# Two stacked blocks on one core: the norms' sums on VectorE, rescaling and broadcasts later in the second block, and the first block's side work in another order

## The chip, the core and the metric

One core of a Trainium2 chip runs the whole program in one launch. Its engines are TensorE (PE in the profile, with its weight loads as PEld), VectorE (DVE), ScalarE (ACT), GpSimd (POOL) and SyncE (SP, which here issues the weight DMAs). Each takes its own instructions strictly in order. The metric is the device time of one execution in microseconds; lower is better. TensorE's clock has two levels in the traces, 1.2 and 2.4 GHz; the profile gives the granted clock of a stretch as a share of the higher one.

## The reference

Two different blocks of two layers each work on one sequence of 256 tokens with 1024 features. Everything is fp32.

```python
def first_block(x, ...):
    for i in range(DEPTH):                       # 2 layers
        h = rmsnorm(x, norm_mix[i])
        q, k, v, cb, cc, cx, u, g = jnp.split(h @ w_in[i], IN_SPLITS, axis=-1)
        y_attn = sliding_window_attention(rope(q), rope(k), v, attn_sinks[i]) @ w_attn_o[i]
        y_conv = (cb * short_conv(cc * cx, conv_w[i])) @ w_conv_o[i]
        ys = gelu(s5_ssm(u, ...))
        y_ssm = (ys * sigmoid(ys @ w_ssm_glu[i])) @ w_ssm_o[i]
        gates = sigmoid(g + b_gate[i]).reshape(b, l, 3, D_MODEL)
        x = x + (gates[0] * y_attn + gates[1] * y_conv + gates[2] * y_ssm) @ w_mix_o[i]
        gt, up = jnp.split(rmsnorm(x, norm_ffn[i]) @ w_ffn_in[i], 2, axis=-1)
        x = x + (silu(gt) * up) @ w_ffn_out[i]
    return rmsnorm(x, norm_final)

def second_block(x, ...):
    for l in range(DEPTH):                       # 2 layers
        h = rmsnorm(h_in, norm_mix_w[l]) @ w_in[l]   # q, k, v, g_ret, z, xbc, dt, gates
        # retention: 4 heads, 256 keys, 512 values, rotary; rms norm per head, times silu(g_ret)
        # ssd: causal conv of width 4, silu, chunked scan over 4 groups of 8 heads,
        #      times silu(z), rms norm per group
        # merged = sigmoid(gate_ret) * o_ret + sigmoid(gate_ssd) * o_ssd;  h += merged @ w_o[l]
        # h += swiglu(rmsnorm(h, norm_ffn_w[l]))
    return rmsnorm(h, final_norm_w)
```

## The kernel before

**Products.** The activations stand in `X` with features on partitions (8 tiles of 128 features by 256 tokens). Each fp32 product is made of three products in a rounded format: a weight chunk of 512 KB lands as `raw`, ScalarE rounds it to `wh` (`cp`), VectorE subtracts to get the rest `wl` (`sub`), and the input is split likewise into `xh` and `xl`, which lie in one tile `xhl`. `fm` gives a result with features on partitions (24 matmuls with 256 columns for a chunk of four 128-row pieces), `tm` one with tokens on partitions. `raw` has 4 buffers, `wh` and `wl` 5 together, PSUM has 4 `mm` tiles for products, 3 `ax` tiles for everything else and one `st` tile.

**Norms.** `Norm` spares a wait for the norm: the products after it run on `X` times the gain, without the factor of the token. `pair(mp)` makes `xhl` for two feature tiles as soon as they are known, and `squares(mp)` squares them on ScalarE (tile `sq`) and adds the two halves into `acc`. `steps` sums `acc` over partitions on TensorE into `st`; rsqrt on VectorE, in some fourteen instructions of 128x2, gives `rsc` (a factor for each token, tokens on partitions); `rowbc` spreads it along the free dimension: VectorE writes a diagonal `dg`, TensorE multiplies it by ones into an `ax` tile, ScalarE copies that to `rsb`. Results made before that are scaled when they leave PSUM. `rescale` later makes a new `xhl` from `X` times `rsb`, so that the rest of the products need no factor: four muls of 128x512 (tile `sq`), each with two roundings on ScalarE and two on VectorE. In six norms `acc` is added on POOL for `mp` 0 to 2 (five adds of 128x256) and on VectorE for `mp` 3; in the first one all are on VectorE.

**First block.** `layer1` runs over `w_in`: two `fm` for `u` (of the S5), a `tm` for k and v, in whose middle (`mid_kv`) the norm is finished and `spread_u` copies the scaled `u` into `U2` with 32 copies of 32x128, half of them on ScalarE and half on VectorE; a `tm` for q; `rescale`; for each half of the conv branch `pc_`, `px` and `pb`; then gates, the S5 output, attention, and `w_mix_o`. Between products `bg.tick` advances a side list. In layer 0 that is `PLAN_0`, the making of the S5 tables for four groups b: `A1`, `A2` (powers of the state's rotation, on POOL, into tile `W`), `PC`, `CP` (powers on VectorE into tile `CP`), `BP` (POOL), `BX` (ScalarE copies `BP` into a padded tile `BX` and `CP` into `W`), `WK` (transposes of `BX`, two `ax` tiles, copied into `W`; then 16 small products of `W` by `BX` into a third `ax` tile), `KK` (16 copies of that into `W`), `M1` (the state products and the scan) and `M2` (the output `py` in an `ax` tile, then a tanh form of gelu: a square on ScalarE, two steps on VectorE, a tanh on ScalarE, and `Y` on VectorE, which frees `py`). The tables of layer 1 (`PLAN_1`) are made beside the feed-forward part of layer 0, and the scheduler may begin them earlier.

**Second block.** In `layer2` each of four heads has products for q, k and v, then one for `sg` (`silu2`: a tanh and a multiply), and `head_tail` later. Head 0's q, k and v run without the norm's factor, then `rescale`, then `sg`. The ssd part ends each of four groups with a norm over the group: rsqrt and `rowbc` again.

**Order.** Code order sets each engine's order, but a list scheduler moves what has a priority: `high_priority(offset=URGENT)`, with URGENT = 200, lets the instructions written inside it go ahead by that many. `pinned` keeps what it is given in code order, behind the last instruction of each engine that it finds in a look back:

```python
for i in reversed(seq[-300:]):
    last.setdefault(i.engine, i)
```

The lines that a reader needs: L104 is `tt` (all two-input steps of VectorE and POOL), L116 the two-step form of VectorE, L119 `ts`, L129 `act` (all of ScalarE), L135 `mmu`, L790 the memset of a `W` tile, L828 the transposes of `WK`.

## Time and profile before

| what | value |
|---|---|
| median of 3 runs | 2252.89 us (2251.32 to 2256.33) |
| profiled execution | 2256.99 us, span 2255.2 us |
| mean granted TensorE clock | 0.986 |
| PE busy | 2178.6 us, 97% |
| DVE busy | 1548.2 us, 69% |
| ACT busy | 1221.7 us, 54% |
| POOL busy | 199.6 us, 9% |
| HBM read | 386.88 MB, 175 GB/s over the span |

The times in the rows are counted from the start of the span. A matmul's own time in a row includes its way through the pipeline, so neighbours overlap; how fast they follow each other is read from a stretch, as its length over the count. A group such as "x4" is several instructions one after the other, with their time together. A wait names the engine and the tile whose event came last.

### The profile page before, as it was taken

The page shows a single profiled execution, that of the slowest core. Times are in us where ns is not written, and L with a number is a line of the kernel's source. Part 1 is how long each engine was busy: PE and PEld are TensorE (multiplying, and loading weights), DVE is VectorE, ACT ScalarE, POOL GpSimd, SP SyncE. Part 2 cuts the span into 40 slices and gives each one's busy share as a digit, 9 for nine tenths or more (in the row PEclk, how much of TensorE's full clock was granted, in tenths as well). Part 3 has the DMA queues.
Part 4 walks back from the last instruction along what each step waited for, and adds up shares of the span by engine and source line. Part 5 has one row for each costly group of instructions (what it writes and reads, how often), then busy time and mean ns, then how long its engine had stood idle before and what let it go on. Part 6 is the DMA issues. An engine that isn't in the chain of part 4 may idle for free. (4 is left out here: it accounts for less than half of the span.)

```text
span 2255.2 us, 36864 instructions
## 1 busy us (share of the span) xinstructions
PE 2178.6 (97%) x14368; PEld 1971.0 (87%) x14368; DVE 1548.2 (69%) x2515; ACT 1221.7 (54%) x1949; POOL 199.6 (9%) x359
## 2 busy tenths in 40 slices
PE   7999969999999999999999999999999999999997
PEld 6898958899999889888999989889888899989886
DVE  7766646568756655776568887556766668887554
ACT  6666537645555444444476755444444477655442
POOL 5810244001000000100000000000100000000000
PEclk9899989999999999999999999999999999999999
DMA  6443537766645655555566646555555566456553
GB/s 184 148 127 122 168 120 240 233 207 220 195 136 178 191 186 173 162 186 165 160 201 202 187 157 192 186 174 183 171 166 177 161 200 199 149 185 196 185 178 103
DMA packets 343935, 397.75 MB, mean 176 GB/s; under 512 B 27988, under 2 KB 276688, under 8 KB 342736
## 3 DMA queue, kind: packets, MB, share of 16 engines
q1 hardware_dynamic: 342816, 394.48, 56.0%
q8 instruction: 113, 1.85, 0.3%
q10 hardware_dynamic: 592, 0.79, 0.1%
q14 instruction: 62, 0.51, 0.1%
q0 software_dynamic: 352, 0.11, 0.0%
HBM read 386.88 MB, written 8.45 MB: 175 GB/s over the span
## 5 line engine op out<-in xcount | busy, mean ns | idle before, releaser
L104 DVE TENSOR_TENSOR wl<-raw,wh 128x1024 fp32r<-128x1024 f32 (+1 forms) x698 | 850.1, 1221 | 516.5 <-ACT wh L129 488.4
L129 ACT ACTIVATE wh<-raw 128x1024 fp32r<-128x1024 f32 (+1 forms) x698 | 727.8, 1047 | 822.5 <-PE mm L135 663.4
L135 PE MATMUL mm<-xhl,wh 128*128 128x256 f32 x3616 | 672.2, 287 | 4.9 <-ACT xhl L129 3.2
L135 PE MATMUL mm<-wh,xhl 128*128 128x512 f32 (+1 forms) x2176 | 645.3, 381 | 3.0 <-DVE xhl L116 1.3
L135 PEld LDWEIGHTS mm<-xhl,wh 128*128 128x128 f32 x3616 | 567.7, 192 | 11.5 <-ACT xhl L129 4.1
L135 PE MATMUL mm<-xhl,wl 128*128 128x256 f32 (+1 forms) x1808 | 515.3, 285 | 3.8 <-DVE wl L104 3.8
L135 PEld LDWEIGHTS mm<-wh,xhl 128*128 128x128 f32 x2176 | 398.7, 190 | 81.3 <-issue 4.3
L135 PE MATMUL mm<-wl,xhl 128*128 128x512 f32 (+1 forms) x1088 | 410.4, 377 | 5.5 <-DVE wl L104 5.5
L135 PEld LDWEIGHTS mm<-xhl,wl 128*128 128x128 f32 (+1 forms) x1808 | 347.6, 192 | 5.7 <-DVE wl L104 4.9
L135 PEld LDWEIGHTS mm<-wl,xhl 128*128 128x128 f32 x1088 | 206.8, 190 | 43.2 <-DVE wl L104 6.0
L135 PE MATMUL mm<-hh,wh 128*128 128x512 f32 (+1 forms) x660 | 185.4, 348 | 0.0
L135 PE MATMUL mm<-y,wh 128*128 128x512 f32 (+1 forms) x576 | 182.1, 372 | 1.0 <-DVE y L116 1.0
L135 PE MATMUL mm<-hh,wl 128*128 128x256 f32 x528 | 147.9, 280 | 0.0
L135 PE MATMUL mm<-y,wl 128*128 128x256 f32 x512 | 144.3, 282 | 0.0
L135 PEld LDWEIGHTS mm<-hh,wh 128*128 128x128 f32 x660 | 114.7, 188 | 16.7
L135 PEld LDWEIGHTS mm<-y,wh 128*128 128x128 f32 x576 | 103.8, 188 | 21.9 <-DVE y L116 1.7
L104 POOL TENSOR_TENSOR acc<-sq 128x256 f32<-128x256 f32 x6 | 4.8, 795 | 1245.3 <-ACT sq L129 1245.3
L135 PEld LDWEIGHTS mm<-hh,wl 128*128 128x128 f32 x528 | 99.1, 188 | 0.0
L135 PEld LDWEIGHTS mm<-y,wl 128*128 128x128 f32 x512 | 96.2, 188 | 0.5 <-issue 0.3
L135 PE MATMUL mm<-mg,wh 128*128 128x256 f32 x512 | 90.5, 280 | 0.0
L135 PEld LDWEIGHTS mm<-mg,wh 128*128 128x128 f32 x512 | 78.4, 189 | 0.0
L116 DVE SCALAR_TENSOR_TENSOR ta<-mm,vec,ta 128x255 f32<-128x255 f32 (+2 forms) x144 | 67.2, 476 | 9.5 <-ACT ta L129 9.2
(363 smaller groups left out, 2446.6 us busy)
## 6 DMA issues: line engine op xcount, KB each, us to landing
raw<-in_w_in_dram SPq DMA_DIRECT2D x284, 512.0 KB, 4.3
raw<-in_w_ffn_in_dram SPq DMA_DIRECT2D x88, 512.0 KB, 3.6
raw<-in_w_gate_up_dram SPq DMA_DIRECT2D x88, 512.0 KB, 3.5
raw<-in_w_down_dram SPq DMA_DIRECT2D x42, 512.0 KB, 3.8
raw<-in_w_ffn_out_dram SPq DMA_DIRECT2D x40, 512.0 KB, 3.5
raw<-in_ret_out_dram SPq DMA_DIRECT2D x32, 512.0 KB, 3.8
raw<-in_ssd_out_dram SPq DMA_DIRECT2D x32, 512.0 KB, 3.4
raw<-in_w_mix_o_dram SPq DMA_DIRECT2D x16, 512.0 KB, 3.4
```

Of the source, the lines that this page charges most:

```text
L104: return eng.tensor_tensor(out=o, in0=a, in1=b, op=op)
L116: return V.scalar_tensor_tensor(out=o, in0=a, scalar=s, in1=b, op0=op0, op1=op1)
L129: return SC.activation(out=o, in_=i, func=f, **kw)
L135: return PE.matmul(out=o, lhsT=l, rhs=r, start=start, stop=stop)
```

## The change

Several things change together.

1. `squares` adds all of `acc` on VectorE.
2. At the start a tile `warm` of 128x256 zeros feeds twelve fp32 matmuls into an `ax` tile that nobody reads, ahead of the transposes of the input.
3. In `layer1` the chunks of q's product are given a priority of 250 ahead. `mid_kv` spreads only the first half of `u`; the second half is scaled into a part of `Y2` and spread after the first half of the conv branch. `pc_` of the first half runs on the unscaled `xhl`, and `rsb` is multiplied in when it leaves PSUM; `rescale` and (in layer 0) `params_1` come behind it.
4. `BXs` copies all of `BP` to `BX` first and then `CP` to `W`; the 16 small products go from `WK` to `KK`.
5. The first gate product of the attention branch runs before attention, and the later ones one step earlier; the attention's second pool has two buffers instead of one.
6. In `layer2` head 0's `sg` runs before `rescale`: the tanh takes the factor of the token, and the rest of it goes into `rd` of `head_tail`.
7. The Exp of `al` is pinned, and `pinned` looks back over 2000 instructions instead of 300.
8. In the group norms of the ssd the rsqrt is urgent, and `rowbc` lets one more step pass between `dg` and its product.

```diff
-        for i in reversed(seq[-300:]):
+        for i in reversed(seq[-2000:]):
...
-    def chunk(parts, kn, n):
+    def chunk(parts, kn, n, ahead_by=0):
...
-        for ap, off in parts:
-            nc.sync.dma_start(out=raw[:, :, off:off + ap.shape[1]], in_=ap.rearrange("(k p) c -> p k c", p=128))
-        cp(wh, raw)
-        sub(wl, raw, wh.bitcast(F32))
+        with tc.high_priority(offset=ahead_by):
+            for ap, off in parts:
+                nc.sync.dma_start(out=raw[:, :, off:off + ap.shape[1]], in_=ap.rearrange("(k p) c -> p k c", p=128))
+            cp(wh, raw)
+            sub(wl, raw, wh.bitcast(F32))
...
-    def rowbc(colv, o):
+    def rowbc(colv, o, wait=False):
...
         yield
+        if wait:
+            yield
...
-            eng = V if mp == 3 or self.gain is gfirst else G
             if mp == 0:
                 self.acc = T(sqp, [128, S], "acc")
-                add(self.acc, sq[:, 0], sq[:, 1], eng)
+                add(self.acc, sq[:, 0], sq[:, 1])
             else:
                 for k in range(2):
-                    add(self.acc, self.acc, sq[:, k], eng)
+                    add(self.acc, self.acc, sq[:, k])
...
-            for ri in range(2):
-                t, x = W2[:, ri], z[:, ri]
-                for a in range(2):
-                    r = slice(64 * a, 64 * a + 64)
-                    cp(t[r, :, :, a, :], CP[r, :, ri].rearrange("p i t h -> p t i h"), -1.0 if ri else None)
-                    cp(x[r, :, :, a, :], BP[r, :, ri].rearrange("p i t h -> p t i h"))
+            halves = [(ri, a, slice(64 * a, 64 * a + 64)) for ri in range(2) for a in range(2)]
+            for ri, a, r in halves:
+                cp(z[r, ri, :, :, a, :], BP[r, :, ri].rearrange("p i t h -> p t i h"))
+            for ri, a, r in halves:
+                cp(W2[r, ri, :, :, a, :], CP[r, :, ri].rearrange("p i t h -> p t i h"), -1.0 if ri else None)
...
+        def KK(b):
+            W2, KT = st[b]["w"][1:3]
             pk = axt([128, 128])
...
-        def KK(b):
-            KT, kk = st[b]["w"][2], st[b]["kk"]
...
-        ap2 = st.enter_context(tc.tile_pool(name="att2", bufs=1))
+        ap2 = st.enter_context(tc.tile_pool(name="att2", bufs=2))
...
-            for m2 in range(2):
-                spread_u(m2)
+            scale_u(0)
+            spread_u(0)
+            scale_u(1)
...
-        ps = tm(w, 0, D, XX, mid=lambda: bg.tick(next(steps)))
+        ps = tm(w, 0, D, XX, mid=lambda: bg.tick(next(steps)), ahead_by=250)
...
-        nm.rescale(V if l == 0 else G)
...
-            cp(z, pc_)
+            if m2 == 0:
+                mul(z, pc_, bc(nm.rsb, 2))
+                nm.rescale(V if l == 0 else G)
+            else:
+                cp(z, pc_)
             bg.tick(next(steps))
+            if m2 == 0 and l == 0:
+                pinned(params_1)
...
+            if m2 == 0:
+                spread_u(1)
...
+        g0 = gate(0, 0, p=inner.enter_context(tc.tile_pool(name="g0p", bufs=1)))
...
-            g = gate(0, mp)
+            g, g0 = g0, gate(0, mp + 1) if mp < 3 else None
...
-            act(al, al, AF.Exp)
+            pinned(lambda: act(al, al, AF.Exp))
...
-            ts(rd, rd, 0.5, None, ALU.mult, ALU.bypass)
+            if h == 0:
+                stt(rd, rd, 0.5, nm.rsc, ALU.mult, ALU.mult)
+            else:
+                ts(rd, rd, 0.5, None, ALU.mult, ALU.bypass)
...
+            pg = tm(w, 4096 + 512 * h, D, XX, mid=bg.tick)
             if h == 0:
+                rh = T(sm, [128, 2], "r8")
+                ts(rh, nm.rsc, 0.5, None, ALU.mult, ALU.bypass)
+                silu2(pg, sg, rh)
                 nm.rescale()
-            sg = e["sg"] = T(r2, [128, 2, 512], "sg")
-            silu2(tm(w, 4096 + 512 * h, D, XX, mid=bg.tick), sg)
+            else:
+                silu2(pg, sg)
...
-            rd = rsqrt(ps[:, 0:2], 2, 1.0 / 512)
+            with tc.high_priority(offset=URGENT):
+                rd = rsqrt(ps[:, 0:2], 2, 1.0 / 512)
...
-            yield from rowbc(rd, rdb)
-            yield
+            yield from rowbc(rd, rdb, True)
...
-    warm = ip.tile([128, 1], F32, name="warm")
+    warm = ip.tile([128, 256], F32, name="warm")
     V.memset(warm, 0.0)
-    act(warm, warm, AF.Exp)
+    act(warm[:, 0:1], warm[:, 0:1], AF.Exp)
+    idle = axt()
+    for _ in range(12):
+        mmu(idle[:, 0, :], warm[:, 0:128], warm, True, True)
```

**Where instructions go.** On POOL, before, near the end of layer 0's `w_mix_o`, the adds of its second norm stood between the steps of layer 1's S5 tables (`g`, `BP`, `W`):

```order
L104 TENSOR_TENSOR g_554_3684<-bt_3548,s_cw 128x256
L104 TENSOR_TENSOR g_555_3685<-bt_3548,s_cw 128x256
L104 TENSOR_TENSOR BP_3683<-g_554_3684,g_555_3685 128x4x64
L104 TENSOR_TENSOR acc_3315<-acc_3315,sq_3383 128x256
L104 TENSOR_TENSOR g_554_3684<-bt_3548,s_cw 128x256
L104 TENSOR_TENSOR acc_3315<-acc_3315,sq_3383 128x256
L104 TENSOR_TENSOR g_555_3685<-bt_3548,s_cw 128x256
L104 TENSOR_TENSOR BP_3683<-g_554_3684,g_555_3685 128x4x64
L790 MEMSET W_3695 128x1792
```
After, on VectorE, the same adds stand between the weight rests `wl`, the residual update of `X` and the rounding rests of `xhl`:

```order
L116 SCALAR_TENSOR_TENSOR X<-mm_3402,X 128x512
L104 TENSOR_TENSOR wl_3665<-raw_3663,wh_3664 128x1024
L116 SCALAR_TENSOR_TENSOR xhl_92<-X,vec,xhl_92 128x256 x2
L104 TENSOR_TENSOR acc_3330<-acc_3330,sq_3468 128x256 x2
L104 TENSOR_TENSOR wl_3683<-raw_3681,wh_3682 128x1024
L116 SCALAR_TENSOR_TENSOR X<-mm_3472,X 128x512
L104 TENSOR_TENSOR wl_3775<-raw_3773,wh_3774 128x1024
L116 SCALAR_TENSOR_TENSOR xhl_92<-X,vec,xhl_92 128x256 x2
L104 TENSOR_TENSOR acc_3330<-acc_3330,sq_3538 128x256 x2
L104 TENSOR_TENSOR wl_3793<-raw_3791,wh_3792 128x1024
```
All of them now follow the `xhl` step of their own pair of tiles, and the last two have one `wl` in front of the next rsqrt.

On VectorE, before, in layer 0's product for q, the rest of its last weight chunk (`wl_801`) stood behind the second half of the copies to `U_48_386` and steps of `params_1` (`vec`, `hbg`, `gfm`), and the muls of `rescale` (`sq`) followed:

```order
L1051 COPY U_48_386<-ta_619 32x2x64 x7
L218 COPY vec<-ax_689 128x128
L104 TENSOR_TENSOR g_103_736<-CP_674,s_pw 128x256
L119 TENSOR_SCALAR hbg<-vec 128x48
L104 TENSOR_TENSOR gfm<-vec 128x8
L104 TENSOR_TENSOR gf_108<-vec 128x8
L104 TENSOR_TENSOR g_104_737<-CP_674,s_pw 128x256
L104 TENSOR_TENSOR wl_801<-raw_799,wh_800 128x1024
L104 TENSOR_TENSOR CP_674<-g_103_736,g_104_737 128x4x64
L104 TENSOR_TENSOR sq_821<-X,rsb_508 128x512
```
After, that last chunk is `wl_790`, and it stands ahead of the norm's `dg`, while the scaling of `u` (`ta_614`) comes behind:

```order
L104 TENSOR_TENSOR wl_790<-raw_788,wh_789 128x1024
L116 SCALAR_TENSOR_TENSOR s_hs<-s_hs 128x32
L104 TENSOR_TENSOR nt_506<-nt_506,nv_503 128x2
L119 TENSOR_SCALAR s_hs<-s_hs 128x32
L116 SCALAR_TENSOR_TENSOR ny_505<-nt_506,ny_505 128x2
L476 COPY rsc_502<-ny_505 128x2
L119 TENSOR_SCALAR dg_522<-C,rsc_502 128x128 x2
L119 TENSOR_SCALAR r_93_685<-rsc_502 128x2
L116 SCALAR_TENSOR_TENSOR s_u<-s_hs 128x32
L116 SCALAR_TENSOR_TENSOR s_x<-s_hs 128x32
L104 TENSOR_TENSOR s_pw<-s_mag,s_u 128x32
L104 TENSOR_TENSOR ta_614<-mm_401,rsb_521 128x2x64x4
```
The four `wl` of q have moved in front of the broadcast, and the copies and `params_1` behind the conv product's weights.

On ScalarE, before, in layer 0, the copies for the second S5 group into `W_744` and `BX_515` alternated:

```order
L129 ACTIVATE ta_1203<-mm_1142 128x512
L129 ACTIVATE W_744<-CP_1085 64x20x16
L129 ACTIVATE BX_515<-BP_677 64x16x16
L129 ACTIVATE W_744<-CP_1085 64x20x16
L129 ACTIVATE BX_515<-BP_677 64x16x16 x3
L129 ACTIVATE wh_1531<-raw_1530 128x1024
L129 ACTIVATE W_744<-CP_1085 64x20x16 x2
```
After, all copies into `BX_528` stand ahead of those into `W_733`, and three weight roundings (`wh`) stand before the square `n` of the group before, where two and the conv step `tb` stood:

```order
L129 ACTIVATE ta_1215<-mm_1154 128x512
L129 ACTIVATE BX_528<-BP_673 64x16x16 x4
L129 ACTIVATE W_733<-CP_1081 64x20x16 x2
L129 ACTIVATE wh_1493<-raw_1492 128x1024
L129 ACTIVATE W_733<-CP_1081 64x20x16 x2
L129 ACTIVATE wh_1543<-raw_1542 128x1024
L129 ACTIVATE wh_1577<-raw_1576 128x1024
L129 ACTIVATE n_185_1300<-ax_1287 128x256
```
The first copy into `BX` no longer stands behind a copy that needs `CP`.

## Rows read from the trace of the kernel before

**Rows 1.** The page's busy time by engine and its groups, `busy, mean ns`.
```profile
PE 2178.6 (97%) x14368; PEld 1971.0 (87%) x14368; DVE 1548.2 (69%) x2515; ACT 1221.7 (54%) x1949; POOL 199.6 (9%) x359
...
L104 DVE TENSOR_TENSOR wl<-raw,wh 128x1024 fp32r<-128x1024 f32 (+1 forms) x698 | 850.1, 1221 | 516.5 <-ACT wh L129 488.4
```
**Rows 2.** TensorE's waits: line <- releaser: us in total, times, longest us.
```profile
PE st L135 <- DVE acc L104: 16.9, 1, 16.9
PE mm L135 <- DVE wl L104: 9.3, 6, 5.5
PE ax L135 <- DVE dg L119: 8.3, 5, 3.2
PE ax L135 <- ACT W L129: 6.5, 3, 3.0
...
PE mm L135 <- ACT xhl L129: 3.2, 2, 2.6
PE mm L135 <- ACT ss L129: 2.0, 1, 2.0
...
PE mm L135 <- DVE xhl L116: 1.3, 2, 0.8
```
**Rows 3.** Stretches: us, busy us (x) of PE PEld DVE ACT POOL, PEclk, DMA, GB/s.
```profile
10.00:20.00 10.00, 9.14 (x53) 8.84 (x54) 9.01 (x15) 9.44 (x17) 0.00 (x0) 1.00 1.02 250
20.00:30.00 10.00, 10.00 (x85) 9.88 (x84) 8.71 (x37) 7.04 (x11) 0.00 (x0) 1.00 0.77 244
40.00:50.00 10.00, 4.46 (x15) 3.33 (x14) 9.83 (x25) 4.65 (x14) 9.45 (x21) 0.70 0.14 43
50.00:60.00 10.00, 8.48 (x43) 7.00 (x42) 8.70 (x15) 8.05 (x17) 9.42 (x21) 0.79 0.33 106
90.00:100.00 10.00, 5.43 (x41) 4.94 (x42) 9.24 (x16) 9.17 (x17) 8.99 (x20) 0.76 0.75 237
100.00:110.00 10.00, 10.00 (x73) 9.64 (x65) 3.73 (x5) 8.98 (x26) 6.51 (x12) 0.73 0.10 30
190.00:200.00 10.00, 10.00 (x68) 9.39 (x68) 5.42 (x18) 5.25 (x8) 0.00 (x0) 0.83 0.39 124
280.00:290.00 10.00, 10.00 (x64) 8.84 (x63) 6.72 (x8) 4.33 (x8) 9.30 (x19) 1.00 0.64 205
300.00:310.00 10.00, 2.88 (x9) 2.50 (x10) 3.69 (x10) 0.00 (x0) 5.75 (x12) 0.50 0.06 15
310.00:320.00 10.00, 10.00 (x38) 8.07 (x37) 5.78 (x17) 4.45 (x5) 0.00 (x0) 0.82 0.47 148
```
**Rows 4.** Timeline around 290 us: start, us, instruction, [idle before <-releaser].
```profile
293.32 0.63 ACT L129 ACTIVATE sq<-X 128x512 f32<-128x512 f32 x1 [6.81 <-POOL acc L104]
...
304.62 1.52 POOL L104 TENSOR_TENSOR acc<-acc,sq 128x256 f32<-128x256 f32 x2
...
306.18 0.89 DVE L104 TENSOR_TENSOR acc<-acc,sq 128x256 f32<-128x256 f32 x2 [17.64 <-POOL acc L104]
```
**Rows 5.** Timeline from 45 to 66 us: VectorE, POOL and TensorE.
```profile
45.67 1.63 DVE L104 TENSOR_TENSOR wl<-raw,wh 128x1024 fp32r<-128x1024 f32 x1
...
47.83 1.59 POOL L790 MEMSET W<- 128x1792 f32 x1
...
64.98 0.65 PE L135 MATMUL ax<-W,BX 128*32 128x128 f32 x16
```
**Rows 6.** Timeline of the S5 steps: ScalarE and TensorE near 91, VectorE at 128 us.
```profile
90.34 0.47 ACT L129 ACTIVATE W<-CP 64x320 f32<-64x320 f32 x1 [4.80 <-DVE CP L104]
...
91.96 2.00 PE L828 MATMUL ax<-C,BX 128*128 128x128 f32 x8 [1.55 <-ACT BX L129]
...
128.53 0.42 DVE L116 SCALAR_TENSOR_TENSOR Y<-n,ax 128x256 f32<-128x256 f32 x1 [0.48 <-ACT n L129]
```
**Rows 7.** Timeline of the second block, layer 1: ScalarE and TensorE.
```profile
1586.65 0.23 ACT L129 ACTIVATE al<-al 128x32 f32<-128x32 f32 x1 [4.34 <-DMA al<-in_a_log_dram]
...
1938.59 1.22 PE L135 MATMUL ax<-dg,C 128*128 128x128 f32 x4 [3.21 <-DVE dg L119]
```

35 lines of the change are left out of this document (19 added, 16 removed).

## The prediction

> **What bounds the kernel now.** I read the busy shares first. TensorE is busy for 2178.6 of 2255.2 us [rows 1], so a change that leaves its matmuls alone can give back only two things: the time in which TensorE stands still, and the time in which it runs at 1.2 GHz instead of 2.4. The first is in the view of TensorE's waits by releaser [rows 2]: one wait of 16.9 us for VectorE's `acc`, six for `wl` with 9.3 us together, five for `dg` with 8.3, three for ScalarE's `W` with 6.5, and so on, some 60 us in all. The second is in the stretches of 10 us [rows 3]: a slice with a granted clock of 0.83 lost 0.17 x 10 = 1.7 us of full-speed work if TensorE was busy. Four slices read 0.83 (190, 230, 950 and 1610 us; one row stands for them); the first 110 us and 300 to 320 us are worse. Everything else on VectorE, ScalarE and POOL counts only where one of these waits ends on it.
>
> The profiled execution took 2256.99 us, 4.1 us above the median of 2252.89. I sum against 2256.99 and then move the forecast part of the way to the median.
>
> **The change part by part.**
>
> *Norms' sums on VectorE.* TensorE asks for the sum of squares of layer 0's second norm and waits 16.9 us [rows 2]; VectorE's last adds end at 306.18 + 0.89 = 307.07 [rows 4], so TensorE asked near 290.2. ScalarE's last square could have started at 286.5 but waited 6.81 us for a buffer that POOL's adds held, and POOL's last two adds came at 304.62, behind the S5 tables of the next layer; VectorE waited 17.64 us for them [rows 4]. Then TensorE ran at half clock: the slice 300 to 310 has it busy for 2.88 us at 0.50 (1.4 us lost), the next reads 0.82 (1.8 lost) [rows 3]. So 16.9 + 3.2 = 20.1 us hang on this one place. After the change the square ends near 287.2, and two adds at 0.44 each (0.89 for two [rows 4]) end before 290.2 even behind one more `wl` of 1.2 us [rows 1]. I take **-20.1**. What is late next is nothing on POOL: its tables lose the adds from their queue. The bill is five adds in each of six norms, 30 x 0.44 = 13 us more on VectorE, which is busy for 6.7 of 10 us where these adds fall (slice 280 to 290 [rows 3]); I price them at nothing there.
>
> A VectorE instruction beside POOL work is longer in this trace: the `wl` at 45.67 took 1.63 us against a mean of 1.22 [rows 1, 5]. By that the two last adds cost 0.4 us more each, inside the slack. The Trainium skill ("SBUF — State Buffer", section "Who interferes with whom") is harsher on this move: an instruction of VectorE with two inputs in SBUF and a POOL instruction that reads SBUF shut each other out for a whole instruction. By that each add could stand behind a whole POOL add (0.76 us, half of the 1.52 for two [rows 4]), the sum would be about 1.5 us late at worst, and the gain here 18.6 instead of 20.1.
>
> *The start.* Twelve matmuls on a zeroed tile now run first. Their price has no row; the four fp32 products with 128 columns at 1938.59, with the clock still low, took 1.22 us [rows 7], so one with 256 columns takes an estimated 0.61 at most and the twelve 7.3 us. They can push the first transposes back by up to 3.5 us. On the other side, the slice 10 to 20 with 53 matmuls in 9.14 us (0.172 each) could run like the next with 85 in 10 (0.118) [rows 3]: 53 x 0.054 = 2.9 us. But VectorE and ScalarE are at 9.0 and 9.4 there. And what this gains or loses is taken in by the wait at 50 us, below. I take **0**, with -2.5 to +3.5.
>
> *First conv product before the rescaling, q's weights first.* The longest `wl` wait (5.5 us) is q's last weight chunk: its `wl` starts on VectorE at 45.67 [rows 5], behind sixteen spreading copies and the table work. With the smaller waits up to 53 us (0.7 and 0.7) and the slices at 0.70 and 0.79 (about 1.3 lost in the first, where TensorE mostly stood, 2.1 in the second) this stretch costs 10 us. Now all four `wl` stand ahead of `dg`, half of the copies come later, and the conv product runs on unscaled input. What is late next is the second conv product, which wants rescaled input: ScalarE's copies into `W` wait for POOL's memset (47.83 + 1.59 = 49.4 us [rows 5]), four at 0.47 us [rows 6] end at 51.3, and only then come the rounded halves, with two weight roundings of 1.05 between them. So the last arrive near 57.5, and with half of the product (24 matmuls) to do then, TensorE ends it near 60.5. Before, it had those 24 still ahead behind the `W` by `BX` product at 64.98 [rows 5], which makes 64.98 + 0.65 + 24 x 0.118 = 68.5: **-8** (-3 if it stands there twice at half clock, -11 if POOL comes earlier).
>
> *S5 side work.* For the second of the four S5 groups TensorE waited 1.55 us for `BX`, because a `W<-CP` copy ahead of it on ScalarE waited 4.80 us for VectorE's powers [rows 6], and then 3.0 us, with the clock at 0.76 and 0.73 [rows 3] (2.4 lost in part, and 2.7): 9 us together. The copies to `BX` now go first, so the first wait goes. The second, put down to `W`, is as near to the buffer that VectorE's `Y` frees: the same wait one group later ends right behind the `Y` at 128.53 + 0.42 [rows 6]. That chain (ScalarE's square, VectorE, a tanh behind four `W` copies and three weight roundings) is not shortened; TensorE only has 24 matmuls to do before it instead of 15 or 13, that is 9 to 11 x 0.118 = 1.1 to 1.3 us more cover. I expect 3 us of waiting left in the first case with some half clock: -4.5; of the two others (6.5 - 3.0 = 3.5 together [rows 2]) the added cover takes 2.3. **-6.8** (-2 to -11.5).
>
> *Gate product ahead of attention.* The wait for `ss` (2.0) and the 0.83 slice behind it (1.7) now have 48 matmuls in front, 5.7 us of cover: **-3.7**. In attention the second buffer and the gate product one step earlier take part of the `o` and `PT` waits and of another 0.83 slice: **-1.5**.
>
> *Second block.* `v`, then a rescaling, then head 0's gate product: TensorE waits for VectorE's `xhl` once in each layer (1.3 us in both [rows 2]) and loses 1.7 in a 0.83 slice each time. The gate product now runs unscaled, and its scale goes into the tanh and the later norm factor. 1.3 + 3.4: **-4.7**. The rescaling follows chunk by chunk while that product runs. The hoisted Exp of `al` waited 4.34 us for its DMA in front of a weight rounding and `xhl` [rows 7]; TensorE's longest wait for ScalarE's `xhl` is 2.6 us [rows 2]. Pinned, it stands later: **-2.5**. For `dg` (five waits, 8.3 us, one of 3.21 with the clock still low after it [rows 2, 7]) the urgent rsqrt moves `dg` forward only by a few small instructions in two groups of three, since the same six `wl` remain ahead of it; in the third two fewer remain and TensorE asks later. **-3** of the 8.3, and as much as all of it and another 1.7 of clock if I misread the queue.
>
> Sum: 20.1 + 0 + 8 + 6.8 + 3.7 + 1.5 + 4.7 + 2.5 + 3 = 50.3, so 2256.99 - 50.3 = 2206.7; from the median it would be 2202.6. I forecast **2205**.
>
> **The rivals.**
>
> *First block gives nothing.* The work there is bound by POOL and ScalarE rather than by their order: POOL is at 9.4 of 10 us from 40 to 60 [rows 3], and both new places (the memset, the tanh chain) are waits that the change doesn't shorten. Against it: `wl` at 45.67 is a matter of order alone. Then only the norm's 20.1, the second block's 4.7 and 2.5 and half of the 3 for `dg` are left: 28.8, 2228 us. Chance 0.17.
>
> *The sums don't come free.* The change may not do what it says at 290 us if ScalarE's square is late by itself. Its wait names POOL, which speaks against it. If the place gives back half, 10 us less: 2215. Chance 0.06.
>
> *Slower: VectorE falls behind in the norm stretches.* The adds sit in front of `wl` on the same queue, at three steps in each of six norms. If at each of these 18 places the 0.9 us of two adds make TensorE wait so that its clock falls, the price of a place is about that of the wait at 92 us and a 0.83 slice, 1.5 + 1.7 = 3.2, so 58 us: 2205 + 58 = 2263. It decides from the point where VectorE has under 0.9 us to spare in a step; it has 3.3 in 10 us [rows 3], so it would need nearly all 18. Chance 0.02.
>
> **How the numbers follow.** Forecast 0.75, the three rivals 0.17, 0.06 and 0.02. The range: at the upper end the first block fails (2228). At the lower end the three uncertain terms come out at half of their distance to their best (8 to 9.5, 6.8 to 9, 3 to 6.5, start -1) and the forecast starts from the median: 2202.6 - 8.2 = 2194; below it I leave some room: 2190 to 2228. Faster by over 0.2% (4.5 us, about what a measurement of this kernel can tell from no change): 0.96; slower 0.02; the same 0.02.
>
> **What would show it.** In the profile after, the `acc` wait should be under 1 us and the slices 290 to 320 at clock 1.00, with no `acc` row on POOL. The longest `wl` wait should be gone, and a wait for `xhl` should stand near 50 us. A wait of about 3 us should stand at the second `W` by `BX` product, with `BX` gone from the waits. `dg` should still be among them, with some 5 us. The prediction is wrong if the first block's slices keep their clocks, or if VectorE's `wl` waits grow in the norm stretches.

## The result and the profile after

The changed kernel takes 2214.26 us (median of 4 runs, 2211.83 to 2216.40); the kernel before took 2254.61 us beside it (4 runs, 2251.32 to 2256.79). The ratio is 0.982 (0.980 to 0.984): 40.4 us or 1.8% faster. The forecast was 2205 with a range of 2190 to 2228. So the side and the range were right, and 9 us of the gain did not come. The profiled execution took 2215.61 us, with a span of 2213.8 us.

The page's busy times and TensorE's waits in the kernel after answer to [rows 1, 2] (a wait: line <- releaser, us in total, times, longest us):

```profile
PE 2168.3 (98%) x14392; PEld 1962.3 (89%) x14392; DVE 1549.8 (70%) x2549; ACT 1220.4 (55%) x1947; POOL 187.3 (8%) x329
```

```profile
PE mm L135 <- DVE wl L104: 11.4, 6, 7.2
PE mm L135 <- ACT xhl L129: 7.9, 1, 7.9
PE ax L135 <- DVE dg L119: 3.6, 6, 1.0
PE ax L135 <- ACT warm L129: 2.7, 1, 2.7
PE mm L135 <- DVE xhl L116: 1.3, 3, 0.8
PE ax L135 <- ACT U L129: 1.2, 1, 1.2
```

The `acc` wait of 16.9 is gone, `W` and `ss` are gone, and `dg` went from 8.3 to 3.6. But `wl`, of which the longest wait should have vanished, rose from 9.3 to 11.4 with a longest of 7.2, and `xhl` from ScalarE rose from 3.2 to 7.9. The stretches of the kernel after answer to [rows 3] (us, busy us (x) of PE PEld DVE ACT POOL, PEclk, DMA, GB/s):

```profile
40.00:50.00 10.00, 9.23 (x58) 8.21 (x57) 9.76 (x25) 2.76 (x6) 9.29 (x26) 1.00 0.25 77
50.00:60.00 10.00, 2.06 (x16) 1.79 (x14) 1.39 (x2) 6.91 (x16) 9.42 (x24) 0.78 0.25 82
60.00:70.00 10.00, 8.84 (x51) 8.44 (x51) 10.00 (x18) 7.57 (x16) 9.45 (x14) 0.71 0.08 20
70.00:80.00 10.00, 10.00 (x97) 9.67 (x96) 9.83 (x18) 4.76 (x12) 9.42 (x24) 1.00 0.51 156
80.00:90.00 10.00, 5.33 (x45) 5.12 (x43) 9.33 (x13) 7.08 (x17) 8.68 (x11) 0.99 0.35 103
90.00:100.00 10.00, 7.51 (x48) 7.52 (x49) 8.66 (x14) 5.68 (x11) 0.00 (x0) 0.67 0.57 177
100.00:110.00 10.00, 10.00 (x99) 9.67 (x98) 7.93 (x12) 8.18 (x17) 6.80 (x19) 1.00 0.63 193
190.00:200.00 10.00, 9.88 (x80) 9.31 (x78) 8.32 (x17) 7.67 (x13) 0.00 (x0) 1.00 0.75 230
290.00:300.00 10.00, 10.00 (x49) 8.30 (x48) 9.86 (x16) 5.11 (x9) 9.73 (x16) 1.00 0.49 163
300.00:310.00 10.00, 10.00 (x50) 8.36 (x49) 7.79 (x11) 8.40 (x14) 9.30 (x18) 1.00 0.66 205
```

At 290 to 310 us TensorE is full at full clock, where it stood or crawled before. At 190 us the slice at 0.83 is gone. At 40 us TensorE gained 4.8 busy us, and at 50 us it lost 6.4: the hole has moved by one slice and is no smaller. VectorE, busy for 8.70 in the slice from 50 us before, now has 1.39, and then 10.00 in the next.

Where the time went is read best from the start of the same matmul in both traces:

| matmul | before | after | difference | step | forecast of the step |
|---|---|---|---|---|---|
| first product by `dg` | 31.78 | 33.14 | +1.4 | +1.4 | 0 |
| first product of `U` by `W` (conv and q done) | 71.29 | 74.35 | +3.1 | +1.7 | -8 |
| fourth one (last S5 group) | 162.71 | 163.99 | +1.3 | -1.8 | -6.8 |
| start of `w_mix_o` (gate, attention done) | 262.00 | 256.51 | -5.5 | -6.8 | -5.2 |
| product by `dg` of the second norm | 321.82 | 296.68 | -25.1 | -19.6 | -20.1 |
| product by `dg` of the second block's first norm | 943.06 | 918.23 | -24.8 | +0.3 | 0 |
| end of the second block | 2243.93 | 2202.53 | -41.4 | -16.6 | -10.2 |

The second norm's step came within half a microsecond. The first 164 us should have given 14.8 us and gave a loss of 1.3. The second block gave 6.4 more than forecast.

**The place that failed.** These are the instructions of the kernel after in order of time (start, us, engine, instruction, [idle before <-releaser]), from POOL's table chain to the two long waits:

```profile
35.48 0.29 POOL L104 TENSOR_TENSOR c<-s_u 128x32 f32<-128x32 f32 x1 [1.75 <-DVE s_u L119]
...
44.79 1.49 POOL L104 TENSOR_TENSOR c<-s_rot 128x32 f32<-128x32 f32 x2
46.24 1.23 POOL L104 TENSOR_TENSOR s_rot<-s_rot,c 128x32 f32<-128x32 f32 x1
...
52.18 0.72 POOL L104 TENSOR_TENSOR BP<-g,g 128x256 f32<-128x256 f32 x1
```

```profile
52.94 0.84 ACT L129 ACTIVATE BX<-BP 64x256 f32<-64x256 f32 x2 [7.88 <-POOL BP L104]
...
57.19 1.90 ACT L129 ACTIVATE W<-CP 64x320 f32<-64x320 f32 x4
59.12 1.71 ACT L129 ACTIVATE xhl<-sq,gfirst 128x256 fp32r<-128x256 f32 x4
```

```profile
59.66 1.42 DVE L116 SCALAR_TENSOR_TENSOR xhl<-sq,gfirst,xhl 128x256 fp32r<-128x256 f32 x3 [8.61 <-ACT xhl L129]
```

```profile
59.68 1.10 PE L135 MATMUL mm<-xhl,wh 128*128 128x256 f32 x2 [7.94 <-ACT xhl L129]
...
92.48 0.58 PE L135 MATMUL mm<-xhl,wl 128*128 128x256 f32 x1 [7.16 <-DVE wl L104]
```

And POOL and ScalarE in the kernel before:

```profile
31.34 0.53 POOL L104 TENSOR_TENSOR c<-s_u 128x32 f32<-128x32 f32 x2 [21.36 <-issue]
...
43.98 0.79 POOL L104 TENSOR_TENSOR BP<-g,g 128x256 f32<-128x256 f32 x1
...
44.80 0.84 ACT L129 ACTIVATE BX<-BP 64x256 f32<-64x256 f32 x2 [1.64 <-POOL BP L104]
```

The reader is to follow one chain. POOL's first `BP` comes 8.2 us later than before (52.18 against 43.98). ScalarE's copy of it into `BX`, at the head of its group as it was before, makes all of ScalarE wait for 7.88 us instead of 1.64; behind it stand two more `BX`, the `W` copies and only then the rounding of the rescaled input, though VectorE's first two `sq` had ended at 49.85. TensorE waits 7.94 us for that `xhl`. VectorE stands 8.6 us behind the same rounding and then has more to do than time: 10.00, 9.83 and 9.33 busy in the three slices from 60 us. At the end of that stretch TensorE waits again, 7.16 us for a `wl`. Both waits are followed by half clock. While it lasted, three matmuls took 0.64 us from start to start of the next three (60.79 to 61.43 us) against 0.36 at full clock (68.20 to 68.56), so 44% of the 6.1 us from 59.7 to 65.8 is lost, 2.7 us, and some 1.8 after the second wait. In all, 7.9 + 2.7 + 1.2 (a smaller `wl` wait at 68 us) + 7.2 + 1.8 = 20.8 us, about the 19 that the two stretches at 40 and at 90 us had cost before.

### The profile page after: what moved, and what is told of

Same layout as the page of the kernel before. It is cut to its first block, busy times and chain, and to the rows that moved or that the text cites. A ratio compares the mean times of both kernels' runs of the same rounds, so it can differ in the third digit from the quotient of the medians.

```text
span 2213.8 us, 36878 instructions
## 1 busy us (share of the span) xinstructions
PE 2168.3 (98%) x14392; PEld 1962.3 (89%) x14392; DVE 1549.8 (70%) x2549; ACT 1220.4 (55%) x1947; POOL 187.3 (8%) x329
## 4 chain that ended last, share of the span: by engine, by line
PE 81%; DVE 6%; ACT 6%; DMA 4%; issue 1%; POOL 1%; SPq 0%; ACTq 0%; DVEq 0%; POOLq 0%
PE mm L135 73%; PE ax L135 6%; ACT Lm L129 2%; DMA Lm<-acd 2%; DMA raw<-in_w_in_dram 2%; DVE wl L104 2%; ACT wh L129 1%; PE ax L568 1%; DVE Lm L104 1%; DVE ta L116 0%; ACT ta L129 0%; ACT W L129 0%; DVE xhl L116 0%; DVE m L104 0%; PE ax L1382 0%
## 5 line engine op out<-in xcount | busy, mean ns | idle before, releaser
L135 PE MATMUL mm<-xhl,wl 128*128 128x256 f32 (+1 forms) x1808 | 514.1, 284 | 11.4 <-DVE wl L104 11.4
L104 POOL TENSOR_TENSOR sq<-X,rsb 128x512 f32<-128x512 f32 x12 | 21.5, 1800 | 1186.3 <-ACT rsb L129 1149.1
```

The costliest lines, as they stand in the source:

```text
L104: return eng.tensor_tensor(out=o, in0=a, in1=b, op=op)
L135: return PE.matmul(out=o, lhsT=l, rhs=r, start=start, stop=stop)
```

## Experiments

Parts are numbered as in the section on the change. "mg" is the start of `w_mix_o` (256.51 us in the kernel after, 262.00 before): what the parts do to layer 0 of the first block up to there has happened by then. A kernel with a single run (no interval) is read by such positions, not by its total. Positions differ between executions too: two kernels below (e_old_rescale2 and e_no_urgent) have the first block's code of the kernel after and start `w_mix_o` at 258.87 and 256.78, so a difference of up to some 2.4 us at mg says little by itself.

**The sums alone (e_sums_only)**, on the kernel before:

```diff
-            eng = V if mp == 3 or self.gain is gfirst else G
+            eng = V
```

> The kernel before with one edit: all of Norm's adds on VectorE, nothing else. Theory (the wait of 16.9 us for acc and the 3.2 us of half clock behind it are POOL's queue alone): 20 us off, about 2234.5 us against 2254.6, no acc wait near 290 us, the rest of the trace shifted as a whole. Rival (ScalarE's square is late by itself): 10 us off, an acc or sq wait of some 7 us stays. Rival (VectorE falls behind in the norm stretches): new wl waits there and less than 15 us off.

2232.42 us, ratio 0.989 (0.987 to 0.991). The product by `dg` of the second norm starts 19.9 us earlier than before, and the distance stays at 19.8 up to the second block's first norm. VectorE's last two adds and the product that needs them in this kernel:

```profile
288.25 1.58 DVE L104 TENSOR_TENSOR acc<-acc,sq 128x256 f32<-128x256 f32 x2
```

```profile
290.37 0.50 PE L135 MATMUL st<-C,acc 128*128 128x1 f32 x4
```

The adds end at 289.83 and TensorE, which had asked near 290.2 by the prediction, does not wait. The term of 20.1 is shown by itself. The total is 24.3 us better than the kernel before, though; the other 4.5 us arise in the second block, where this kernel changes nothing that TensorE waited for. Before, the clock fell there after three waits (950, 1610 and 1938 us), 5 us in all at 1.7 a piece. Here are the slices with the first two of these places, which come 20 us earlier in this kernel:

```profile
930.00:940.00 10.00, 9.03 (x38) 6.82 (x38) 10.00 (x17) 5.88 (x10) 3.56 (x2) 1.00 0.18 54
1590.00:1600.00 10.00, 10.00 (x44) 8.00 (x43) 10.00 (x12) 5.39 (x8) 3.55 (x2) 1.00 0.36 103
```

The waits for `xhl` are still there (0.56 and 0.79 us), and the clock did not fall. So the 1.7 us is no fixed price of such a wait: in one trace half clock follows it, in the next it doesn't. The median of the four runs lies as low as the profiled one, though, so the gain in the second block is not that execution alone; what makes it stays open.

**Without the twelve matmuls (e_no_warm)**, on the kernel after:

```diff
-    idle = axt()
-    for _ in range(12):
-        mmu(idle[:, 0, :], warm[:, 0:128], warm, True, True)
```

> The changed kernel without the twelve matmuls on zeros at the start. In the changed kernel they wait 2.7 us for ScalarE's Exp on the same tile and push the first transposes from 4.9 to 10.8 us; the first product is 2.1 us later than before, and its end of the u products 2.0 us later. Theory (they cost 2 us, since ScalarE and the loads set the pace of the first products and not the clock; POOL's chain hangs on VectorE's s_u and starts 2 us earlier without them): the sum of squares of the first norm is asked for 2 us earlier (near 22.3 us), 2 us less in all, about 2212. Rival (the warm clock pays for the delay): the u products then end at 24 us or later as they run at half clock, and the time is the same or up to 1 us longer.

2213.02 us, 0.981 (0.979 to 0.983), not to be told from the kernel after. The first norm's sum starts 1.9 us earlier, but the product by `dg` at 33.12 us against 33.14, and mg at 256.9. The start's term of 0 holds. Both long waits stay, 8.01 and 7.22 us, so they do not come from the start. The theory of 2 us less is not borne out: what the start gives is gone by mg.

**BX one entry later (e_bx_late)**, on the kernel after:

```diff
-PLAN_0 = ("A1:0 A2:0", "PC:0 A1:1", "CP:0 A2:1", "", "BX:0", "", "WK:0",
+PLAN_0 = ("A1:0 A2:0", "PC:0 A1:1", "CP:0 A2:1", "", "", "BX:0", "WK:0",
```

> The changed kernel with one entry of the first block's side list moved: BX:0 (ScalarE's copies from POOL's BP to BX and into W) one step later, so that the rescaled input's roundings stand ahead of them on ScalarE. In the changed kernel TensorE waits 7.9 us for xhl at 51.7 us while ScalarE waits 7.9 us for POOL's BP in front of it. Theory (the order on ScalarE makes the wait, POOL's late chain only sets its length): the wait for xhl falls under 2 us, the half clock from 55.6 to 65.8 goes, and 8 to 14 us are saved, about 2202 to 2206, unless WK then waits for BX. Rival (this stretch is bound by POOL whatever stands in the queue): the wait moves on to the transposes of BX with about the same length and the time is within 3 us of 2214.

2209.62 us, 0.979 (0.977 to 0.980); mg at 251.06, 5.45 us earlier than in the kernel after. ScalarE's first rounding, and TensorE's waits in the stretch:

```profile
50.80 1.69 ACT L129 ACTIVATE xhl<-sq,gfirst 128x256 fp32r<-128x256 f32 x4
```

```profile
53.55 0.39 PE L135 MATMUL mm<-xhl,wh 128*128 128x256 f32 x1 [1.57 <-DVE xhl L116]
...
94.63 0.64 PE L135 MATMUL ax<-W,BX 128*32 128x128 f32 x16 [2.66 <-POOL BP L104]
...
115.77 0.58 PE L135 MATMUL mm<-xhl,wl 128*128 128x256 f32 x1 [3.80 <-DVE wl L104]
```

With the copy behind the rounding, the rounding starts 8.3 us earlier and the 7.94 us wait is 1.57. So ScalarE's order behind a late POOL made that wait, not POOL's lateness alone. The gain is less than the 8 to 14 us that were expected. It is the fastest version found, but e_old_conv and e_bx_spread below come within 1.4 us of it, and its interval and that of the kernel after meet at 0.980.

**Part 3 undone (e_old_conv)**, on the kernel after: `rescale` ahead of the conv branch, `params_1` ahead of q, both halves of `u` spread in `mid_kv`, no priority for q.

```diff
-            if m2 == 0:
-                mul(z, pc_, bc(nm.rsb, 2))
-                nm.rescale(V if l == 0 else G)
-            else:
-                cp(z, pc_)
+            cp(z, pc_)
...
-        ps = tm(w, 0, D, XX, mid=lambda: bg.tick(next(steps)), ahead_by=250)
+        ps = tm(w, 0, D, XX, mid=lambda: bg.tick(next(steps)))
```

> The changed kernel with its part 3 undone: q's chunks without priority, both halves of u spread in the middle of k and v, params_1 ahead of q, and the rescaling ahead of the first conv product as in the kernel before. My prediction gave this part 8 us: about 2222. Theory now (in the changed kernel the part gives nothing, as q's wait of 5.5 us has become a wait of 7.9 us for xhl and one of 7.2 us for wl): within 4 us of 2214, with q's wl wait of about 5 us back and the two new waits gone.

2210.12 us, 0.979 (0.978 to 0.981); mg at 250.76, 5.75 us earlier than with part 3. The part that was to give 8 us costs 4 (by the medians) to 6 us (by mg) beside the others. The `xhl` wait is still there, one product earlier, so part 3 alone does not make it:

```profile
54.17 1.31 PE L135 MATMUL mm<-xhl,wh 128*128 128x256 f32 x4 [8.56 <-ACT xhl L129]
```

Its slices show what differs: VectorE stands for 2.2 of the 10 us from 50 us on, not for 8.6, and TensorE is full from 60 to 90 us. The long `wl` wait near 92 us is gone with VectorE's standstill.

```profile
50.00:60.00 10.00, 5.16 (x21) 4.81 (x22) 7.79 (x13) 8.91 (x21) 9.65 (x16) 0.50 0.19 52
60.00:70.00 10.00, 10.00 (x77) 10.00 (x76) 7.69 (x10) 6.10 (x9) 9.53 (x13) 0.88 0.79 240
80.00:90.00 10.00, 10.00 (x85) 10.00 (x85) 9.96 (x15) 7.12 (x12) 9.49 (x17) 1.00 0.40 112
```

**Part 3 undone and BX later (e_conv_bx)**: both edits above.

> The changed kernel with part 3 undone (rescaling ahead of the first conv product, both halves of u spread in one go, no priority for q) and BX:0 one step later in the side list. Each edit alone took the start of w_mix_o from 256.5 us to about 251. Theory (both waits of 8 us for xhl are ScalarE's copies waiting for POOL's BP in front of the roundings; the second wait of 7 us for wl is part 3's copies on VectorE): the xhl wait near 46 us shrinks from 8.6 to 1 to 4 us and w_mix_o starts at 243 to 248 us, the time is 2203 to 2208. Rival (the first block is bound by POOL's chain, so the two edits remove the same time): w_mix_o starts at 250 to 252 us and the time is about 2210.

2215.73 us, 0.982 (0.979 to 0.985); mg at 253.37. The two gains do not add up: the `xhl` wait is 3.93 us, but three more of about 3 us (2.94, 3.07 and 2.75) appear, for `xhl` and `wl` from VectorE. Neither expectation named this. Either edit alone ends the pile-up on VectorE; why both together bring waits of their own stays open.

**All four BX later (e_bx_all)**: in `PLAN_0` `BX:1`, `BX:2` and `BX:3` are put one entry later too.

> The changed kernel with BX:0 to BX:3 all one entry later in the first block's side list (the run before moved only BX:0 and took the start of w_mix_o from 256.5 to 251.1 us). Theory (what stays of the first block's waits, 2.7 us for W by BX and 3.8 us for wl with half clock behind it, comes from ScalarE's copies of the next groups waiting for POOL in front of other work): w_mix_o starts at 244 to 249 us, the time is 2203 to 2208 and clearly below the changed kernel. Rival (POOL's chain of BP sets these waits): w_mix_o starts at 250 to 253 us, the time is 2208 to 2211.

2214.46 us, 0.982 (0.980 to 0.984); mg at 253.37. The wait near 50 us is 1.59, but TensorE waits 2.07 us for `W` at the second group (2.66 for `BP` in e_bx_late) and 2.27 at the fourth, where e_bx_late has no such wait. One entry later helps the first group, where POOL is late; that it helps the others is not seen, and the time lies outside both expectations.

**Part 4 undone (e_old_s5)**: `BXs`, `WK` and `KK` as before (the edit to `BXs` is shown).

```diff
-            for ri, a, r in halves:
-                cp(z[r, ri, :, :, a, :], BP[r, :, ri].rearrange("p i t h -> p t i h"))
-            for ri, a, r in halves:
-                cp(W2[r, ri, :, :, a, :], CP[r, :, ri].rearrange("p i t h -> p t i h"), -1.0 if ri else None)
+            for ri in range(2):
+                t, x = W2[:, ri], z[:, ri]
+                for a in range(2):
+                    r = slice(64 * a, 64 * a + 64)
+                    cp(t[r, :, :, a, :], CP[r, :, ri].rearrange("p i t h -> p t i h"), -1.0 if ri else None)
+                    cp(x[r, :, :, a, :], BP[r, :, ri].rearrange("p i t h -> p t i h"))
...
```

> The changed kernel with its part 4 undone: copies from BP and CP alternate on ScalarE and the small products of W by BX stay in WK. My prediction gave this part 6.8 us. Theory now (part 4 works at its own place, where the waits at W by BX fell from 8.0 us with half clock to 0.7): waits for BX and W come back at the second to fourth group, w_mix_o starts at 262 to 266 us instead of 256.5 and the time is 2220 to 2226. Rival (the waits are only moved, since POOL and VectorE set the pace of the groups): within 3 us of 256.5 and of 2215.

2218.07 us, 0.983 (0.981 to 0.986); mg at 259.21, 2.7 us later than in the kernel after. So part 4 is worth 2.7 us here (3.8 by the medians), not 6.8, and less than was expected of this run too; 2.7 is little more than what two executions can differ by. The `xhl` wait (8.35 us) and a long `wl` wait (5.39) are there without it, and ScalarE still waits 7.88 us for `BP`: in the old order too a copy of it stands ahead of the rounding.

**Both halves of u in one place (e_spread_early)**: the second `spread_u` back in `mid_kv`, with its scaled half in a temporary again; the rest of part 3 kept.

```diff
...
             scale_u(1)
+            spread_u(1)
...
-            if m2 == 0:
-                spread_u(1)
```

> The changed kernel with one piece of its part 3 undone: both halves of u are spread in the middle of k and v; q's priority and the later rescaling stay. Theory (the wait of 7.2 us for wl at 85 us and the half clock behind it come from the second half's copies on VectorE beside the S5 steps of the first group, while the wait of 7.9 us for xhl is the side list's): the xhl wait stays at 7 to 9 us, the wl wait falls under 3 us, w_mix_o starts 4 to 8 us earlier than 256.5. Rival (the wl wait follows from the xhl wait in front of it): it stays at 5 us or more and w_mix_o starts within 2 us of 256.5.

One run: mg at 254.46, 2.05 us earlier, which is within what executions differ by. The copies keep VectorE busy ahead of the wait (4.61 us for `xhl` now), and a `wl` wait of 5.47 us at 85 us remains. The second long wait is thus not made by the later copies alone. That it follows from the time that VectorE lost is borne out by e_bx_late and e_old_conv, in which VectorE doesn't stand so long and that wait is 1.48 us or absent.

**BX later and u in one place (e_bx_spread)**: this edit and that of e_bx_late.

> The changed kernel with BX:0 one entry later in the side list and both halves of u spread in the middle of k and v; q's priority and the later rescaling stay. BX:0 alone brought the start of w_mix_o to 251.1 us, the early spreading alone to 254.5 (from 256.5). Theory (from 60 to 95 us VectorE has no time left over, and each microsecond of copies moved out of that stretch into the one before 50 us comes back to TensorE): w_mix_o starts at 247 to 250 us and the time is 2205 to 2209. Rival (the copies now stand ahead of the conv product's weight rests at 45 us and cost there what they save later): w_mix_o starts at 251 to 253 us and the time is 2209 to 2213.

2210.94 us, 0.980 (0.978 to 0.981); mg at 250.44. No better than e_bx_late: waits of 2.77 and 4.51 us for `wl` (at 45 and 111 us) take the place of its 2.66 for `BP` and 3.80 for `wl`.

**Part 5 undone (e_old_gate)**: the gate product behind attention, one buffer.

```diff
-        ap2 = st.enter_context(tc.tile_pool(name="att2", bufs=2))
+        ap2 = st.enter_context(tc.tile_pool(name="att2", bufs=1))
...
-        g0 = gate(0, 0, p=inner.enter_context(tc.tile_pool(name="g0p", bufs=1)))
...
-            g, g0 = g0, gate(0, mp + 1) if mp < 3 else None
+            g = gate(0, mp)
```

> The changed kernel with its part 5 undone: the attention branch's gate products back in their loop and one buffer in attention's second pool. My prediction gave this part 3.7 + 1.5 = 5.2 us. Theory: the waits for k_tok (1.0) and ss (2.0) come back and one or two half-clock stretches with them, and from the last small product of W by BX to the start of w_mix_o the kernel is 4 to 7 us longer than the changed one, about 2219. Rival (only the waits of 3 us come back, without half clock): 3 us longer.

One run: from the last small product of `U` by `W` to mg 83.33 us against 76.82, so the part is worth 6.5 (forecast 5.2). This way is 83.3 to 83.6 us in the three kernels without the part (before, e_sums_only and this one) and 76.8 or 78.3 in the eleven with it. The wait and the slower slices behind it and in attention are back, as in the kernel before. Three of the eleven (those with 78.3) have a slice near 0.83 in attention too, so only the first slice is the part's alone:

```profile
189.09 0.50 PE L135 MATMUL mm<-ss,wh 128*128 128x256 f32 x2 [2.02 <-ACT ss L129]
```

```profile
190.00:200.00 10.00, 10.00 (x67) 9.49 (x67) 5.41 (x18) 5.47 (x8) 0.00 (x0) 0.83 0.40 113
230.00:240.00 10.00, 9.29 (x64) 8.69 (x64) 4.87 (x7) 3.70 (x5) 0.00 (x0) 0.83 0.18 54
```

**Part 6 undone (e_old_rescale2)**: in `layer2` `rescale` ahead of head 0's `sg`.

```diff
...
-            sg = e["sg"] = T(r2, [128, 2, 512], "sg")
-            pg = tm(w, 4096 + 512 * h, D, XX, mid=bg.tick)
             if h == 0:
-                rh = T(sm, [128, 2], "r8")
-                ts(rh, nm.rsc, 0.5, None, ALU.mult, ALU.bypass)
-                silu2(pg, sg, rh)
                 nm.rescale()
-            else:
-                silu2(pg, sg)
+            sg = e["sg"] = T(r2, [128, 2, 512], "sg")
+            silu2(tm(w, 4096 + 512 * h, D, XX, mid=bg.tick), sg)
```

> The changed kernel with its part 6 undone: in the second block the rescaling again ahead of head 0's gate product. Theory (each layer lost 0.6 to 0.8 us of waiting for xhl and 1.7 us of half clock there): the three waits for tb, v and xhl come back in each layer, and from the norm's dg to the end of the heads each layer is 1 to 2.5 us longer than in the changed kernel, 2 to 5 us together. Rival (the clock falls there or not by chance): less than 1 us a layer, no slice under 1.00.

One run: the `xhl` wait is back (0.55 and 0.78 us, with 0.42 and 0.41 for `v`), and the clock falls at neither place. In layer 0 the way from the norm's `dg` to the merged product is 421.8 us as in the kernel after; in layer 1 that to the first group norm is 289.9 against 288.9, and 288.3 to 289.9 in the kernels that keep parts 6 and 8. So the part is not to be told from nothing, and nothing like 4.7 us comes back: the kernel after has an `xhl` wait of its own (0.33 and 0.78 us), one product later.

**Part 8 undone (e_no_urgent)**: rsqrt without priority, `rowbc` without the extra step.

```diff
-            with tc.high_priority(offset=URGENT):
-                rd = rsqrt(ps[:, 0:2], 2, 1.0 / 512)
+            rd = rsqrt(ps[:, 0:2], 2, 1.0 / 512)
...
-            yield from rowbc(rd, rdb, True)
+            yield from rowbc(rd, rdb)
+            yield
```

> The changed kernel with its part 8 undone: rsqrt of the ssd's group norms without priority, and dg's product one step earlier. Theory of my prediction (the same weight rests stand ahead of dg, so little moves): the dg waits grow by 0.5 to 1.5 us a layer from 3.6 us in all. Rival (the part is what took the waits from 8.3 to 3.6 us and a half clock stretch with it): the waits are back at 7 to 9 us, one of 2 to 3 us with half clock behind it, 5 to 7 us in all.

One run: the same way from `dg` to the merged product grows by 2.8 us in layer 0 (424.6 against 421.8) and by 2.3 in layer 1 (423.6 against 421.3), and no slice there falls below full clock. But the ten kernels here with the second block's code unchanged need 841.8 to 846.9 us for both ways together (mean 844.2, the kernel after 843.1), and this one 848.2. So the part is worth some 4 us, known only to 2 or 3, and by one run. The six waits are 2.10, 0.78, 0.35, 1.52, 1.01 and 1.04 us, 6.8 together against 3.6 in the kernel after and 3.1 to 5.7 in the ten, the longest in this row:

```profile
1210.93 0.71 PE L135 MATMUL ax<-dg,C 128*128 128x128 f32 x4 [2.10 <-DVE dg L119]
```

## Why the prediction was right, and where it was not

Of the signs that the prediction named, the `acc` wait is gone, 290 to 310 us run at full clock, `BX` is gone from the waits, `dg` is left with 3.6 us and an `xhl` wait stands near 50 us. The longest `wl` wait has not gone, and no wait of 3 us stands at the second `W` by `BX` product. By its last sign, the prediction is wrong for the first 110 us: the slices keep their low clocks (0.78, 0.71 and 0.67 where 0.70, 0.79, 0.76 and 0.73 stood). That only 9 of the 16 us missing there show in the total is owed to what gate, attention and the second block gave beyond their terms, and that was luck.

**The norm's sums: right, term and mechanism.** 19.6 us in the kernel after and 19.9 alone, against 20.1. From mg to the second norm's `dg` it is 59.8 us in the kernel before and 39.6 to 40.4 in all thirteen other traces. Nothing was late behind it: in the kernel after the last two adds stand well ahead of the product, which starts without a wait.

```profile
283.02 0.93 DVE L104 TENSOR_TENSOR acc<-acc,sq 128x256 f32<-128x256 f32 x2
```

```profile
285.13 0.50 PE L135 MATMUL st<-C,acc 128*128 128x1 f32 x4
```

POOL was busy for 9.37 of the 10 us around them, and two adds took 0.93 us against 0.89 before. In e_sums_only two adds took 1.58. So the adds can cost VectorE more beside POOL, as the prediction allowed, but in neither kernel did this reach TensorE.

**The start: right in its sum.** The twelve matmuls put the first transposes back by 5.9 us, not by up to 3.5, and the delay was gone at the first `dg`, well ahead of the wait that was to take it in. The 1.4 us that the `dg` product is late are not from the twelve matmuls, since it is as late without them; nor is part 3 the cause (33.61 in e_old_conv), and what is stays open.

**Conv product first: wrong, and this is the step that failed.** The sum took POOL's memset at 49.4 us from the trace of before and hung ScalarE's copies and the roundings on it, as if POOL's chain could not move. In the kernel after, the memset starts at 54.92 and ends at 56.50; the first rounding starts at 59.12, and the second conv product, forecast to end near 60.5, ends near 70.9. Two things moved the chain, and both are effects of the change on the chain's surroundings. First, it begins later: its second input `s_u` comes from VectorE behind `dg` and the scaling of `u`, and POOL's first pair of steps, at 31.34 before, now ends at 35.8; that is about 4 us of the 8.2. Some 2.5 of them hang on the twelve matmuls: without them (e_no_warm) the pair ends at 33.2 and the first `BP` starts at 50.26. TensorE then asks for `xhl` earlier too and waits as long. Secondly, it runs slower: the steps at 44.79 and 46.24 took 1.49 us for two and 1.23 for one, where the same steps before and after them take 0.45 and 0.25 to 0.30. VectorE was then running the `wl` that had been moved forward (44.52, 46.10 and 49.77), where it had run copies of 32 partitions before. That is the other 4 us. Two runs bear it out, with the copies of 32 partitions back in that place. In e_spread_early the chain's second step starts at 35.51, as in the kernel after, and the first `BP` at 49.15, 3.0 us earlier; in e_old_conv it starts later still (36.24), and `BP` at 49.84. The prediction saw the slower `wl` beside POOL, priced it for VectorE and forgot that POOL pays for it as well.

The Trainium skill ("SBUF — State Buffer", "Who interferes with whom") says that an instruction of VectorE with two inputs in SBUF and an instruction of POOL that reads SBUF exclude each other for a whole instruction, and that whichever comes first wins. The trace agrees: POOL's step at 46.24 ends at 47.47, right after the `wl` that ran from 46.10 to 47.35.

The other half of the failure is ScalarE's queue. The prediction had the rounding behind the `W` copies and was right in that, but it did not name the wait of the `BX` copy, which stands at the head of this group with part 4 and without it, as a wait of everything behind it. I had written for the S5 steps "The copies to `BX` now go first, so the first wait goes", and never asked what stood behind that copy in the first group. e_bx_late shows that moving it is worth 5.45 us at mg and 4.6 by the medians.

**S5 side work: the term too large.** The `BX` wait at 92 us did go. The wait foreseen in its place, some 3 us for `W` by `BX` in the second group, is not in the kernel after (what is left of such waits is 0.67 us for POOL's `g`, at 134 us); in its stead the 7.16 us `wl` wait stands at 92 us, made upstream. The positions give 1.8 us and e_old_s5 2.7, of 6.8 forecast, and either is near what executions differ by.

**Gate and attention: right, sized a little low** (6.8 by positions, 6.5 by e_old_gate, 5.2 forecast).

**Second block: the sum too small, and one term wrong.** No run takes back the Exp alone. From layer 0's merged product to layer 1's first `dg` it is 231.1 us in the kernel before, 229.7 in e_sums_only and 228.5 to 228.6 in the twelve kernels with part 7, so it gave 1.1 to 2.5 (2.5 forecast). `dg` gave some 4 (3 forecast). The rescaling gave 0 to 1 instead of 4.7: 3.4 of this was the price of two slices at half clock that are missing in e_sums_only with the same waits in place. I had read what one execution did as the cost of the wait. These and the third such stretch make some 5 of the 16.6 us that the block gave; 2.5 + 4 + 5 leave some 5 us to which no run was given.

**The rivals.** "First block gives nothing" came out half: the 14.8 us of conv and S5 came to a loss of 1.3, as it said, but not for its reason, a bound by POOL and ScalarE rather than by their order: one entry of order (e_bx_late) gives 5.45 us back at mg. Part 5, which it counted as lost too, gave its gain, and the second block brought the total back. "The sums don't come free" and "VectorE falls behind in the norm stretches" fell with e_sums_only. VectorE did fall behind, but at 60 to 92 us, behind a wait of its own.

Taking the parts of the first block apart one at a time gives up to mg +5.75 (part 3), -2.7 (part 4), -6.5 (part 5) and -0.4 (part 2, by e_no_warm): -3.9 against the -5.5 measured. The remaining 1.6 us is what parts do to each other, or what one execution differs from the next by (2.4 us at mg); the runs do not tell these apart.

## What to carry to other kernels

When work is moved forward on one engine, follow every queue on which a result of that stretch depends and ask when each entry would start now; a start time copied from the old trace into the sum is the likeliest error. A copy that waits for a slow engine should stand behind, not ahead of, the work in its queue that is ready, and an engine that is full for the next 30 us can't make up for 8 us lost. A slice at half clock behind a short wait is to be priced only if several executions show it. And before a shift of 2 us is read as the worth of a part, compare the same place in kernels in which nothing was changed there.

## What the runs showed of the hardware

POOL's small steps took three to five times as long beside VectorE's large two-input instructions (two steps 1.49 us against 0.45), while VectorE's `wl` there took 1.25 to 1.27 us, near its mean of 1.22; POOL paid nearly all of it. Beside POOL's steps of 128x256 VectorE can pay as well: in e_spread_early a `wl` at 48.52 took 1.64 us while POOL's `BP` ran from 49.15 to 50.75.

The same short wait is followed by half clock in one execution and not in another. TensorE's product by `U` in layer 1 waits 1.18 to 1.28 us in all fourteen traces. In seven of them a stretch at the lower clock follows, in seven none; from the second norm's `dg` to the second block's first `dg` the former take 623.1 to 623.5 us, the latter 621.2 to 622.0. In the kernel after the next three matmuls by `wh` and `wl` follow at full pace (498.95 to 499.64 us), in e_bx_late at the lower one (493.59 to 494.87):

```profile
496.14 0.83 PE L135 MATMUL ax<-U,W 128*128 128x64 f32 x4 [1.19 <-ACT U L129]
...
498.95 0.62 PE L135 MATMUL mm<-wh,xhl 128*128 128x512 f32 x2
499.40 0.40 PE L135 MATMUL mm<-wl,xhl 128*128 128x512 f32 x1
499.64 0.62 PE L135 MATMUL mm<-wh,xhl 128*128 128x512 f32 x2
```

```profile
490.51 0.83 PE L135 MATMUL ax<-U,W 128*128 128x64 f32 x4 [1.19 <-ACT U L129]
...
493.59 1.05 PE L135 MATMUL mm<-wh,xhl 128*128 128x512 f32 x2
494.44 0.63 PE L135 MATMUL mm<-wl,xhl 128*128 128x512 f32 x1
494.87 1.05 PE L135 MATMUL mm<-wh,xhl 128*128 128x512 f32 x2
```

The twelve fp32 matmuls took 7.9 us from 2.74 us on, and the first transposes came at 10.76 instead of 4.88; by the product of `dg` at 33 us nothing was left of that delay, nor of any gain from it.
